# A two-layer decoder trunk on one core: q and k turned and split for two tiles of tokens at a time, transfers priced by two queues in the planner, pieces and instructions ordered anew

## The chip, the cores and the metric

The kernel runs on one core of one Trainium2 chip. The metric is the device time of one execution in microseconds; each figure for a kernel is the median of its runs. For the kernel before: 1321.85 us, median of 3 runs (1321.65 to 1322.69).

The core has five engines with a queue each, which run in order: TensorE (PE in the profile; its weight loads are PEld), VectorE (DVE), ScalarE (ACT), GpSimd (POOL) and SyncE (SP). TensorE writes PSUM; VectorE and ScalarE read it. Transfers (DMA) are issued here by SP and by POOL.

## What is computed

Two layers over 512 tokens of 1024 channels. Each layer normalises its input, projects it once to twelve parts, and runs two branches side by side:

```python
h = rmsnorm(x, norm_g)
proj = h @ w_in
aq, ak, av, az, bqk, bv, bi, bf, bo, bz, ga, gb = jnp.split(proj, idx, axis=-1)
# A: differential attention, 8 heads, two maps of 64 each, v of 128
q = rope(rmsnorm(two_map_heads(aq), q_norm_g), cos, sin)
k = rope(rmsnorm(two_map_heads(ak), k_norm_g), cos, sin)
oa = diff_attention(q, k, v, lam)            # softmax map 0 - lam * softmax map 1
oa = rmsnorm(oa, attn_norm_g) * (1.0 - lam_init)
ya = (oa * silu(az)) @ w_out_a
# B: mLSTM, 8 heads, q and k of 64 from a causal convolution of 4, v of 128
hb = mlstm_chunkwise(mq, mk, mv, i_pre, f_pre)
yb = (sigmoid(bo) * rmsnorm(hb, mlstm_norm_g) * silu(bz)) @ w_out_b
u = jax.nn.sigmoid(ga) * ya + jax.nn.sigmoid(gb) * yb
return x + u @ w_o
```

## The kernel before

**Products.** Every float32 product is made of three: each operand is split into a rounded high part and the rest (`split`, L522: ScalarE casts, VectorE subtracts), and `mm3` (L526) adds high x high, high x low and low x high in PSUM. Weights come from memory in pieces of 128 x 1024 floats (512 KB). A piece is loaded by SP into `wr`, cast by ScalarE to `wh`, and VectorE makes the rest `wl`. A piece whose name is in the list `dlo` goes another way (`dload`, L1743): POOL loads it into `dh`, ScalarE writes its negative to `dl`, and a second POOL transfer adds the piece onto `dl`. That takes two slots of the pool `qkp` (24 slots); where there is no room, the piece goes the first way. `dla` says how many pieces ahead it is issued.

**Pieces.** Names are those of the parts: qk0 to qk3 (q and k of two heads each, four pieces), av0 and av1, az, ga, bqk, bo, bz, woa, wob (eight each), the gates. bv, gb and wo are made by seven products instead of eight (P1 to P7): for these, combinations of weights are formed by accumulating transfers on POOL or on VectorE (`tdve`, L1736; a sum counts as VectorE's only if the products that it stands between come in a given order), and combinations of the tokens (`lhS`, `llS`) are formed once for bv, written to memory (`dS1h` and so on, L781) and reloaded for gb (L804).

**q and k.** Per pair of heads and tile of 128 tokens, `qk_done` (L1014) takes the sums of squares and rotates into a tile `rot`. At the second tile of a pair of tiles it computes the norms of both and calls `qk_back` and `qk_split` (L1077) for each of the two. `qk_split` queues a step `back`, `qkt` = 5 steps later, which turns the tile with four transposes into one PSUM bank (`qkt`) and takes it apart: `A.copy` of q's half into `qs`, the rest by VectorE, `A.copy` of k's half twice (`ks`), its rest into `kl`. All of these are 64 partitions x 256. `qkn` tells the attention heads how many tiles are there.

**Attention and mLSTM heads** are chains of steps (L1378) with start times (`a0`, `ap`, `m0`, `mp`) and offsets (`attn`, `ml`). A head's first step waits until the head before it has come to step `gateA` or `gateM`. `actp` names the query blocks whose scaling by the softmax sums is ScalarE's, the others are VectorE's. Per head the sum of squares of the output is a product with ones: for heads in `foldA` and `foldM` the two halves of partitions are added first and one product is made (`fold`, L1494), for others the high and low part take two (L1504). The mLSTM steps `decay` and `expm` broadcast rows of gate values from memory (`dd`, `em`).

**Order.** Nothing runs while the kernel is written down: a `Recorder` keeps every operation with its predecessors, and `schedule` (L298) plays them through with prices and picks, engine by engine, the startable operation with the smallest key: its nominal TensorE time, plus a `bias` by the name of its output, plus penalties (`group` for a change between small and large matmuls, `drain`, `late`). SP keeps the recorded order. `issue` (L467) then emits all in that order, which fixes every engine's queue; so every instruction bears L474 in the profile.

The price of a transfer, in nanoseconds, with one line for all queues (`rate`, L288, is in bytes per nanosecond: 360 from memory, 250 from the chip, 175 for rows, 150 accumulating):

```python
go = s + c if e == "POOL" else s
dma = max(dma, go) + size / self.rate(o)
end[i] = max(dma, go) + (5500.0 if e == "POOL" else 5000.0 if o["a"][1].tensor.name.startswith("rows") else 3000.0)
```

## Time and profile before

| | before |
|---|---|
| median of 3 runs | 1321.85 us |
| the profiled execution | 1324.05 us, span 1322.3 us |
| mean granted TensorE clock | 0.999 |
| busy: TensorE, VectorE, ScalarE, POOL | 1310.4, 1068.1, 959.0, 88.7 us |
| moved by DMA | 192.25 MB |

The span runs from the first to the last instruction. A matmul's end is modelled, so a busy TensorE can still be waiting for a short time. Views used below: the table of busy time, busy time in stretches of 33 us, groups of instructions of one operation and tile (count, busy time, mean time of one, idle time of the engine before them and what ended it), the chain of work that ended last (start, duration, what), the timeline, the waits, and the transfers with the median time from issue to landing.

### The profile page before, as it was taken

How to read it: one execution, taken by the hardware profiler on the slowest of the kernel's cores; microseconds unless marked ns; L12 is line 12 of the kernel's file. 1: busy time of each engine (PE TensorE's matmuls, PEld its weight loads, DVE VectorE, ACT ScalarE, POOL GpSimd, SP SyncE). 2: the span in 40 equal slices, each digit the busy share in tenths (PEclk: the TensorE clock that was granted, in tenths of full speed). 3: DMA queues.
4: the chain of work that ended last, by engine and by line, in shares of the span. 5: the costliest groups of instructions: out<-in, count | busy, mean ns of one | idle time of the engine just before them, and what ended most of it. 6: DMA issues, size and time to landing. Idle time of an engine off the chain costs nothing.

```text
span 1322.3 us, 18461 instructions
## 1 busy us (share of the span) xinstructions
PE 1310.4 (99%) x6436; PEld 1096.2 (83%) x6436; DVE 1068.1 (81%) x1890; ACT 959.0 (73%) x1940; POOL 88.7 (7%) x112
## 2 busy tenths in 40 slices
PE   9999999999999999999999999999999999999998
PEld 7888888888888788998888888888888887889886
DVE  7898878797668879967888988788965888797686
ACT  5888789896457768863668887888944677697643
POOL 1000000000010100010100100000001101101100
PEclk9999999999999999999999999999999999999999
DMA  5222232226676557776844222321367655588755
GB/s 189 73 80 83 93 100 74 83 65 175 210 207 167 158 139 185 229 212 146 290 136 123 62 81 82 94 88 58 103 172 253 182 154 143 127 204 275 192 139 191
DMA packets 63373, 192.25 MB, mean 145 GB/s; under 512 B 7440, under 2 KB 14224, under 8 KB 63280
## 3 DMA queue, kind: packets, MB, share of 16 engines
q1 hardware_dynamic: 51184, 147.02, 34.6%
q0 software_dynamic: 12096, 44.05, 15.7%
q8 instruction: 51, 0.84, 0.2%
q14 instruction: 42, 0.34, 0.1%
HBM read 178.39 MB, written 12.65 MB: 144 GB/s over the span
## 4 chain that ended last, share of the span: by engine, by line
PE 89%; DMA 4%; ACT 3%; DVE 2%; issue 1%; SPq 0%; DVEq 0%; ACTq 0%
PE qk L474 13%; PE av L474 9%; PE az L474 7%; PE ga L474 7%; PE woa L474 7%; PE bqk L474 7%; PE wob L474 7%; PE wo_P L474 6%; PE bz L474 5%; PE bv_P L474 5%; PE bo L474 5%; PE gb_P L474 3%; PE sc L474 3%; DMA wr<-in_wp_dram 2%; DMA llS_gb<-dS3l 1%; PE ut L474 1%
## 5 line engine op out<-in xcount | busy, mean ns | idle before, releaser
L474 DVE TENSOR_TENSOR wl<-wr,wh 128x1024 fp32r<-128x1024 f32 (+1 forms) x176 | 209.8, 1196 | 46.4 <-ACT wh L474 41.8
L474 ACT CAST wh<-wr 128x1024 fp32r<-128x1024 f32 (+1 forms) x174 | 181.2, 1043 | 71.9 <-DMA wr<-in_wp_dram 25.6
L474 ACT ACTIVATE p<-sc,mx,rq 128x128 f32<-128x128 f32 (+3 forms) x128 | 78.5, 617 | 11.8 <-DVE mx L474 8.5
L474 PE MATMUL qk<-wl,hh 128*128 128x512 f32 x240 | 85.4, 398 | 0.5 <-DVE wl L474 0.5
L474 PE MATMUL qk<-wh,hl 128*128 128x512 f32 x240 | 84.9, 397 | 0.1
L474 PE MATMUL qk<-wh,hh 128*128 128x512 f32 x240 | 84.2, 397 | 0.8 <-ACT hh L474 0.8
L473 ACT ACT_TABLE_LOAD x61 | 78.3, 1283 | 1.1
L474 PE MATMUL woa<-oa,wh 128*128 128x512 f32 x224 | 72.4, 392 | 0.0
L474 PE MATMUL wob<-ob,wh 128*128 128x512 f32 x192 | 59.5, 390 | 0.0
L474 ACT CAST ks<-qkt 64x256 fp32r<-64x256 f32 x128 | 47.1, 368 | 10.9 <-DVE qs L474 8.7
L474 POOL DMA_DIRECT2D dl<-in_wp_dram x24 | 20.9, 872 | 495.4 <-ACT dl L474 466.5
L474 PEld LDWEIGHTS qk<-wh,hh 128*128 128x128 f32 x240 | 45.4, 189 | 9.7 <-ACT hh L474 1.0
L474 PEld LDWEIGHTS qk<-wl,hh 128*128 128x128 f32 x240 | 45.0, 189 | 9.8 <-DVE wl L474 0.9
L474 PEld LDWEIGHTS qk<-wh,hl 128*128 128x128 f32 x240 | 45.2, 189 | 9.4 <-DVE hl L474 0.4
L474 DVE TENSOR_REDUCE mx<-sc 128x2 f32<-128x256 f32 (+1 forms) x64 | 52.3, 817 | 0.7
L474 PEld LDWEIGHTS woa<-oa,wh 128*128 128x128 f32 x224 | 41.7, 188 | 8.4
L474 DVE SCALAR_TENSOR_TENSOR cv<-bqk,par,cv 128x509 f32<-128x509 f32 (+2 forms) x48 | 35.8, 746 | 13.2 <-ACT cv L474 12.3
L474 PE MATMUL az<-hh,wh 128*128 128x512 f32 x112 | 44.7, 399 | 0.0
L474 ACT ACTIVATE sq<-qk 128x64 f32<-128x64 f32 (+1 forms) x144 | 36.5, 266 | 11.0 <-PE qk L474 10.3
L474 PE MATMUL az<-hh,wl 128*128 128x512 f32 x112 | 44.5, 397 | 0.0
L474 PE MATMUL ga<-hh,wh 128*128 128x512 f32 x112 | 44.4, 396 | 0.0
L474 PE MATMUL az<-hl,wh 128*128 128x512 f32 x112 | 44.4, 396 | 0.0
(400 smaller groups left out, 4147.8 us busy)
## 6 DMA issues: line engine op xcount, KB each, us to landing
wr<-in_wp_dram SPq DMA_DIRECT2D x172, 512.0 KB, 3.6
dh<-in_wp_dram POOLq DMA_DIRECT2D x24, 512.0 KB, 6.4
dl<-in_wp_dram POOLq DMA_DIRECT2D x24, 512.0 KB, 6.7
wws_wo<-in_wp_dram POOLq DMA_DIRECT2D x12, 512.0 KB, 7.4
dd<-rows SPq DMA_DIRECT2D x16, 256.0 KB, 4.1
wws_bv<-in_wp_dram POOLq DMA_DIRECT2D x8, 512.0 KB, 6.8
em<-rows SPq DMA_DIRECT2D x16, 256.0 KB, 7.2
wws_gb<-in_wp_dram POOLq DMA_DIRECT2D x8, 512.0 KB, 10.2
```

Source lines behind the costliest of these rows:

```text
L473: self.tc.keep_in_program_order(self.nc.scalar.preload_act_table_set(self.SET_NAME[o["load"]]))
L474: self.tc.keep_in_program_order(getattr(o["e"], o["fn"])(*o["a"], **o["k"]))
```

## The change

`qk_split` stores a tile and returns; at the second of two it queues two steps, one for q (side 0) and one for k (side 1, one step later). Each turns its half of both tiles by four transposes into one PSUM bank, and each cast or subtraction then covers 64 partitions x 512. `qk_done` and `qk_load` are adapted (`qk_load` isn't used, since `qspill` is empty):

```diff
         def qk_split(c, tt, rq):
+            st[("rot", c, tt % 2)] = rq
+            if tt % 2 == 0:
+                return
+            rqs = [st[("rot", c, t)] for t in range(2)]
+            def back(side):
+                def f():
+                    if side and ("qkq", c, tt) not in st:
+                        return False
+                    pst = ps_tr.tile([P, 2, 2, P], F32, tag="tr", name=f"qkt{side}{l}_{c}_{tt}")
+                    for t in range(2):
+                        for g in range(2):
+                            T.transpose(pst[:, g, t, :], rqs[t][:, (2 * side + g) * P : (2 * side + g + 1) * P], ident)
+                    ts = slice((tt - 1) * P, (tt + 1) * P)
+                    L, H = slice(0, 64), slice(64, 128)
+                    src = pst.rearrange("p g t k -> p g (t k)")
+                    for r, (a, b) in enumerate(((L, H), (H, L))):
+                        t = st[("qs", c)][2 * side + r][:, :, ts]
+                        A.copy(t[a], src[a])
+                        if side:
+                            A.copy(t[b], src[a])
+                            t2_, o = st[("kl", c)][r][:, :, ts], a
+                        else:
+                            t2_, o = t, b
+                        V.tensor_tensor(t2_[o], src[a], t[a].bitcast(F32), ALU.subtract)
...
+            for side in range(2):
+                defer(TUNE["qkt"] + side, back(side))
```

The price of a transfer becomes that of two queues (SP and POOL) that share while both have work:

```diff
         if o["k"].get("accum_op") is not None:
+            return 190.0
+        if o["eng"] == "POOL":
+            return 480.0
+        if src.space == DRAM and src.tensor.name.startswith("rows"):
             return 150.0
-        return 175.0 if src.tensor.name.startswith("rows") else 250.0 if src.space != DRAM else 360.0
+        return 380.0 if src.space == DRAM and math.prod(list(o["a"][0].shape)) >= 131072 else 310.0
+    def land(self, o, go, queue):
...
+        w = size / self.rate(o)
+        own = 0.55 if z else 0.45
+        t = max(go + (100.0 if z else 350.0), queue[z])
+        r = queue[1 - z] - t
+        if r <= 0:
+            fin = t + w
+        elif w / own <= r / (1.0 - own):
+            d = w / own
+            fin = t + d
+            queue[1 - z] = fin + (r - d * (1.0 - own))
+        else:
+            d = r / (1.0 - own)
+            queue[1 - z] = t + d
+            fin = t + d + (w - d * own)
+        queue[z] = fin
+        return fin + (2300.0 if z else 1850.0)
```

The table `TUNE` gets new values: the order of pieces, offsets and penalties, and a new `bias` for nearly every name. Those that change which instructions run, or when heads may start:

```diff
-        "qk0 av0 gate az0 qk1 az1 az2 av1 qk2 az5 ga4 qk3 az3 az4 ga3 az7 ga7 ga6 bqk4 ga2 bqk5 az6 ga1 ga0 woa7 woa3 "
+        "qk0 av0 gate az0 qk1 av1 az1 az2 qk2 az5 ga6 qk3 az3 az4 ga3 az7 ga2 ga0 bqk4 ga5 bqk5 az6 ga7 ga4 woa7 woa3 "
...
-    "attn": (0, 4, 5, 10, 13, 15, 15, 16, 20, 26),
+    "attn": (0, 3, 7, 10, 14, 14, 15, 16, 20, 28),
-    "foldM": (0, 1, 2, 3, 4, 5),
+    "foldM": (1, 3, 4, 5),
-    "gateA": 1,
-    "gateM": 4,
-    "actp": (0, 1, 2, 3),
+    "gateA": 6,
+    "gateM": 1,
+    "actp": (1, 2, 3),
-    "dlo": ('az0', 'az2', 'az6', 'bo1', 'bo4', 'bo6', 'bo7', 'bqk3', 'bz3', 'ga3', 'gb1', 'gb4', 'qk0.3', 'qk1.2', 'woa4', 'wob1', 'wob5'),
-    "dla": 5,
+    "dlo": ('az0', 'az2', 'az3', 'az6', 'bo1', 'bo4', 'bo6', 'bo7', 'bqk3', 'bz3', 'ga3', 'gb1', 'gb4', 'qk0.3', 'qk1.2', 'qk2.0', 'woa0', 'woa4', 'woa6', 'wob1', 'wob5'),
+    "dla": 6,
-    "tdve": {'bv': ('T2', 'T4'), 'wo': ('T1', 'T3'), 'gb': ('T2', 'T4')},
+    "tdve": {'bv': ('T2', 'T4'), 'wo': ('T2', 'T3'), 'gb': ('T2', 'T4')},
-    "group": 2214.6,
+    "group": 524.6,
-    "risk": 182.7,
-    "late": 33.8,
+    "risk": 11511209765781.4,
+    "late": 196689.9,
```

With the new `risk` the penalty `late` falls on every operation alike.

More of the change, by code (lines that the diff above doesn't have):

```diff
@@ L38 @@
     "order": (
[4 rows of a table removed]
[4 rows of a table added]
     ),
     "qkt": 5,
-    "gct": 13,
-    "gls": 2,
-    "glf": 7,
-    "attn": (0, 4, 5, 10, 13, 15, 15, 16, 20, 26),
+    "gct": 11,
+    "gls": 3,
+    "glf": 4,
+    "attn": (0, 3, 7, 10, 14, 14, 15, 16, 20, 28),
     "a0": 24,
@@ L51 @@
     "a4": 20,
-    "ml": (0, 6, 12, 14, 25, 38),
+    "ml": (0, 5, 12, 12, 25, 37),
     "ahead": 3,
-    "lc": 5,
-    "slack": 38.3,
+    "lc": 6,
+    "slack": 175.0,
     "margin": 0.0,
-    "pemargin": 123.8,
-    "wait": 278.0,
+    "pemargin": 140.8,
+    "wait": 208.2,
     "swpen": 141896579.9,
-    "smargin": 466.2,
+    "smargin": 634.6,
     "pwait": 0.0,
-    "wdiff": 6830.8,
+    "wdiff": 6373.2,
     "wsp": 4,
@@ L72 @@
     "acl": 7,
-    "gateA": 1,
-    "gateM": 4,
-    "actp": (0, 1, 2, 3),
+    "gateA": 6,
+    "gateM": 1,
+    "actp": (1, 2, 3),
     "m0": 228,
     "mp": 14,
-    "m4": 6,
+    "m4": 5,
     "slots": 24,
-    "hfd": 20,
+    "hfd": 22,
     "tset": (0, 18),
@@ L88 @@
     "qspill": {},
[3 rows of a table removed]
-    "drain": 62.6,
-    "group": 2214.6,
[3 rows of a table added]
+    "drain": 58.1,
+    "group": 524.6,
     "lates": ('bv', 'gb'),
-    "risk": 182.7,
-    "late": 33.8,
+    "risk": 11511209765781.4,
+    "late": 196689.9,
 }
@@ L291, in rate @@
         if o["k"].get("accum_op") is not None:
+            return 190.0
+        if o["eng"] == "POOL":
+            return 480.0
+        if src.space == DRAM and src.tensor.name.startswith("rows"):
             return 150.0
-        return 175.0 if src.tensor.name.startswith("rows") else 250.0 if src.space != DRAM else 360.0
+        return 380.0 if src.space == DRAM and math.prod(list(o["a"][0].shape)) >= 131072 else 310.0
+    def land(self, o, go, queue):
+        z = int(o["eng"] == "POOL")
+        size = 4.0
+        for x in list(o["a"][0].shape):
+            size *= x
+        w = size / self.rate(o)
[14 more added lines that the diff above has]
+        return fin + (2300.0 if z else 1850.0)
     LAT = {("ACT", "DVE"): 131, ("ACT", "PE"): 262, ("ACT", "ACT"): 153, ("DVE", "ACT"): 130, ("DVE", "PE"): 240, ("DVE", "DVE"): 127,
@@ L343, in schedule @@
         end = [0.0] * n
-        dma = 0.0
+        queue = [0.0, 0.0]
         table = 6
@@ L426, in schedule @@
             if o["fn"] == "dma_start":
-                size = 4.0
-                for x in list(o["a"][0].shape):
-                    size *= x
-                go = s + c if e == "POOL" else s
-                dma = max(dma, go) + size / self.rate(o)
-                end[i] = max(dma, go) + (5500.0 if e == "POOL" else 5000.0 if o["a"][1].tensor.name.startswith("rows") else 3000.0)
+                end[i] = self.land(o, s + c if e == "POOL" else s, queue)
             for t in o["tiles"]:
@@ L1003, in f @@
             def f():
-                if ("qd", c, tt) not in st or tt and st.get(("qkn", c), 0) < tt or not tt and not room(6):
+                if tt % 2 == 0:
+                    return
+                if ("qd", c, tt) not in st or tt > 1 and st.get(("qkn", c), 0) < tt - 1 or tt == 1 and not room(6):
                     return False
-                if not tt:
+                if tt == 1:
                     qk_take(c)
-                rq = t2(f"rl{l}_{c}_{tt}")
-                SY.dma_start(rq, st["qd", c, tt])
-                qk_split(c, tt, rq)
+                for t in (tt - 1, tt):
+                    rq = t2(f"rl{l}_{c}_{t}")
+                    SY.dma_start(rq, st["qd", c, t])
+                    qk_split(c, t, rq)
             return f
@@ L1058, in qk_done @@
             V.tensor_tensor(rqv, y, t, ALU.mult)
+            back = [st[("rot", c, t % 2)] for t in (tt - 1, tt)]
             for t in (tt - 1, tt):
-                qk_back(c, t, st[("rot", c, t % 2)])
+                qk_back(c, t, back[t % 2])
         def qk_back(c, tt, rq):
@@ L1077, in qk_split @@
         def qk_split(c, tt, rq):
-            def back():
-                pst = ps_tr.tile([P, 4, P], F32, tag="tr", name=f"qkt{l}_{c}_{tt}")
-                for g in range(4):
-                    T.transpose(pst[:, g, :], rq[:, g * P : (g + 1) * P], ident)
-                ts = slice(tt * P, (tt + 1) * P)
-                q0, q1, k0, k1 = (t[:, :, ts] for t in st[("qs", c)])
-                kl0, kl1 = (t[:, :, ts] for t in st[("kl", c)])
-                L, H = slice(0, 64), slice(64, 128)
-                for q, k, kl, a, b in ((q0, k0, kl0, L, H), (q1, k1, kl1, H, L)):
-                    A.copy(q[a], pst[a, 0:2, :])
-                    V.tensor_tensor(q[b], pst[a, 0:2, :], q[a].bitcast(F32), ALU.subtract)
-                    A.copy(k[a], pst[a, 2:4, :])
-                    A.copy(k[b], pst[a, 2:4, :])
-                    V.tensor_tensor(kl[a], pst[a, 2:4, :], k[a].bitcast(F32), ALU.subtract)
-                st[("qkn", c)] = tt + 1
@@ L1095, in qk_split @@
-            defer(TUNE["qkt"], back)
+            st[("rot", c, tt % 2)] = rq
+            if tt % 2 == 0:
+                return
+            rqs = [st[("rot", c, t)] for t in range(2)]
[19 more added lines that the diff above has]
+                        V.tensor_tensor(t2_[o], src[a], t[a].bitcast(F32), ALU.subtract)
+                    if side:
+                        st[("qkn", c)] = tt + 1
+                    else:
+                        st["qkq", c, tt] = 1
+                return f
```

10 rows, old and new, of the table TUNE are left out of this document.

## The prediction

> **What bounds the kernel now.** I read the page's table of busy time first, then busy time by stretches of 33 us, then the chain that ended last inside the stretches where TensorE pauses.
>
> ```profile
> span 1322.3 us, 18461 instructions
> PE 1310.4 (99%) x6436; PEld 1096.2 (83%) x6436; DVE 1068.1 (81%) x1890; ACT 959.0 (73%) x1940; POOL 88.7 (7%) x112
> 0.00:33.00 33.00, 29.83 (x125) 23.23 (x126) 24.16 (x67) 19.58 (x47) 4.95 (x9) 0.95 0.56 190
> 33.00:66.00 33.00, 33.00 (x159) 27.37 (x159) 28.22 (x73) 27.78 (x81) 0.00 (x0) 1.00 0.23 73
> 66.00:99.00 33.00, 33.00 (x167) 27.10 (x166) 32.05 (x80) 28.05 (x75) 0.95 (x1) 1.00 0.24 81
> ...
> 363.00:396.00 33.00, 32.66 (x144) 26.42 (x143) 22.52 (x27) 18.45 (x25) 6.18 (x8) 1.00 0.75 205
> 429.00:462.00 33.00, 32.19 (x151) 25.92 (x150) 28.23 (x41) 24.55 (x38) 3.34 (x4) 1.00 0.57 156
> 528.00:561.00 33.00, 32.83 (x235) 30.54 (x234) 30.46 (x43) 30.16 (x42) 1.72 (x2) 1.00 0.75 229
> 561.00:594.00 33.00, 32.67 (x222) 30.30 (x222) 22.57 (x27) 21.97 (x28) 6.36 (x8) 1.00 0.75 216
> ...
> 1023.00:1056.00 33.00, 32.66 (x146) 26.59 (x145) 26.69 (x34) 20.03 (x26) 4.80 (x7) 1.00 0.66 189
> 1089.00:1122.00 33.00, 32.00 (x148) 25.67 (x147) 28.36 (x42) 25.04 (x38) 3.35 (x4) 1.00 0.52 142
> 1188.00:1221.00 33.00, 32.13 (x251) 30.88 (x251) 26.34 (x34) 23.85 (x33) 3.49 (x4) 1.00 0.80 264
> 1221.00:1254.00 33.00, 32.55 (x195) 28.97 (x194) 21.10 (x27) 21.95 (x30) 4.64 (x6) 1.00 0.71 190
> 1287.00:1322.30 35.30, 30.86 (x135) 24.89 (x133) 23.76 (x28) 11.75 (x13) 1.73 (x2) 1.00 0.61 196
> ```
>
> In a stretch's row the first pair after the stretch is TensorE's busy time, the fourth VectorE's (DVE), the fifth ScalarE's (ACT); the last three columns are granted clock, DMA share and GB/s. TensorE bounds: it is idle for 1322.3 - 1310.4 = 11.9 us in all. The rows say where. The first 33 us lose 3.17. The last 35.3 lose 4.44. The eight rows between lose 0.34 + 0.81 + 0.17 + 0.33 + 0.34 + 1.00 + 0.87 + 0.45 = 4.31. All other stretches read 33.00 of 33.00, also 66:99, where VectorE works 32.05 of 33 us: there VectorE is nearly full, and still nothing of it reaches TensorE.
>
> A busy time can hide part of a wait, so the spacing of matmuls matters:
>
> ```profile
> 1294.54 0.50 PE L474 MATMUL wo_P<-wh,uhB 128*128 128x512 f32 x1 [0.78 <-DVE xr L474]
> ...
> 1295.33 0.40 PE L474 MATMUL wo_P<-wh,uhZ 128*128 128x512 f32 x1
> 1295.34 0.19 PEld L474 LDWEIGHTS wo_P<-wl,uhZ 128*128 128x128 f32 x1
> ...
> 1295.57 0.39 PE L474 MATMUL wo_P<-wl,uhZ 128*128 128x512 f32 x1
> ```
>
> A matmul is shown for 0.39 us, but the next starts 0.23 us after it. A wait shows as idle only beyond 0.16 us. The Trainium skill ("Perfetto Trace Analysis", Identifying the Most-Contended Engine) warns that matmul busy share is no measure of headroom, and that the share of weight loads is; by it the 83% would leave 17%, some 220 us. The trace disagrees: a load of 0.19 in a spacing of 0.23 is 0.83 by itself, and in 66:99, with no wait, loads take 27.10 of 33, or 0.82. So 83% is this program's full rate; I give a gain beyond the waits 2 in 100.
>
> What ended the largest of the waits:
>
> ```profile
> 442.33 8.09 DMA wr<-in_wp_dram
> ...
> 451.46 1.53 ACT dd L474 x3
> ...
> 453.01 1.24 DVE dd L474
> ...
> 454.38 0.48 PE ms L474 x2
> 560.90 8.85 DMA llS_gb<-dS3l
> 1184.11 11.07 DMA llS_gb<-dS1l
> 1213.78 9.19 DMA llS_gb<-dS3l
> L474 PE MATMUL gb_P<-llS_gb,wh 128*128 128x256 f32 x128 | 33.4, 287 | 1.4 <-DMA llS_gb<-dS3l 0.8 <-DMA llS_gb<-dS1l 0.6
> 376.77 1.14 DVE llS_bv L474
> ```
>
> A late weight load (wr) held ScalarE's cast; the decay exponentials of an mLSTM head (dd) stood behind that cast, and TensorE waited for them. The same place in layer 1 gives the 1.00 of 1089:1122. The reloaded token combinations llS_gb cost 1.4 us by their own row: 0.33 in 561:594 and 0.45 in 1221:1254 on dS3l, 0.64 of the 0.87 in 1188:1221 on dS1l. So transfers make 0.81 + 1.00 + 0.33 + 0.64 + 0.45 = 3.23 us in five waits; with the hidden 0.16 of each, **4.0 us**. The rest, 0.34 twice at llS_bv, 0.78 at xr and some 0.4 elsewhere, is VectorE's or ScalarE's: 1.9 us, with six hidden parts 2.9.
>
> **The change part by part.** *Turning q and k.*
>
> ```profile
> L474 ACT CAST ks<-qkt 64x256 fp32r<-64x256 f32 x128 | 47.1, 368 | 10.9 <-DVE qs L474 8.7
> L474 ACT CAST qs<-qkt 64x256 fp32r<-64x256 f32 x64 | 23.5, 367 | 11.4 <-PE qkt L474 5.6 <-DVE kl L474 4.5
> L474 DVE TENSOR_TENSOR qs<-qkt,qs 64x256 fp32r<-64x256 f32 x64 | 27.0, 422 | 11.7 <-ACT qs L474 10.3
> L474 DVE TENSOR_TENSOR kl<-qkt,ks 64x256 fp32r<-64x256 f32 x64 | 26.9, 421 | 10.5 <-ACT ks L474 8.9
> L474 ACT ACTIVATE ms_b<-num 64x512 f32<-64x512 f32 x12 | 7.0, 581 | 0.0
> L474 DVE TENSOR_TENSOR mql<-cv,mq 64x512 fp32r<-64x512 f32 x16 | 11.0, 685 | 1.8 <-ACT mq L474 1.3
> ```
>
> The 192 casts and 128 subtractions become 96 and 64 of twice the width. At 0.58 and 0.69 us (the two 64x512 rows) ScalarE goes from 70.6 to 55.7 us and VectorE from 53.9 to 44.2: 15 and 10 us less. The 128 transposes on TensorE stay 128, still four to a PSUM tile. Both engines' savings fall in stretches that read 33.00 of 33.00, so they are worth **0**; the cover is TensorE's own queue. The added wait is small: both tiles of a pair were already queued together, and the k side now stands one step behind the q side. Behind it on TensorE stand the scores of the next head, which the rows show never waited for.
>
> *Smaller edits.* Heads 0 and 2 of the mLSTM are no longer folded before their sum of squares: one matmul more per head and layer, four of 0.23 = **+0.9 us** straight on TensorE, the one certain cost. (It spares VectorE and ScalarE an instruction of 0.58 to 0.69 us in each.) The first scaling of an attention block (0.40 us each, below) goes from ScalarE to VectorE, sixteen times; at most 0.4 x 16 = 6.5 us on VectorE, less than the 10 it is spared: 0, or the whole 6.5 if that were all exposed, which I exclude by 66:99. T1 for T2 in the list for wo does nothing: both need an order of products that wo's sequence doesn't have. Moving av1 right behind qk1 puts two pieces of four accumulators side by side, as qk0 and av0 stand now; 33:66 holds that pair and shows no idle: 0.
>
> *More weights through POOL.* Four more names (az3, qk2.0, woa0, woa6) take the path of two POOL transfers instead of one SP load, a cast and a subtraction: up to 8 pieces in two layers.
>
> ```profile
> L474 ACT ACTIVATE p<-p,sums 128x128 f32<-128x128 f32 x16 | 6.5, 404 | 0.2
> L474 DVE TENSOR_TENSOR wl<-wr,wh 128x1024 fp32r<-128x1024 f32 (+1 forms) x176 | 209.8, 1196 | 46.4 <-ACT wh L474 41.8
> POOL dl L474 <- ACT dl L474: 466.5, 23, 44.2
> wr<-in_wp_dram SPq DMA_DIRECT2D x172, 512.0 KB, 3.6
> dl<-in_wp_dram POOLq DMA_DIRECT2D x24, 512.0 KB, 6.7
> ```
>
> VectorE is spared 8 x 1.2 = 9.6 us, 0 on the path. SP loses 8 loads, POOL gets 16 issues. POOL runs in order, and each accumulation waits there for ScalarE's negated copy, up to 44.2 us; behind it stand the zero fills of kl and mql and the sums for bv, gb and wo. Cost: 0 while those are as early as now; at worst one wait like the largest idle above, 1.0 us, per layer. I take 0, nearest to the 33.00 of the attention stretches. The bytes grow by 8 x 0.5 = 4 MB of 192. The Trainium skill ("DMA: Bandwidth & Descriptors", Issuing engines are not separate DMA queues) says that transfers of all issuers share the same 16 engines, so a second queue brings no rate; that the one row above is nearly twice the other agrees. By this rule the sum would only gain those bytes, spread over both layers.
>
> *The price of transfers in the plan, and the new order.* This alone can touch the 4.0 us. The planner sets every engine's order from prices. The old price runs all transfers in one line and adds 3.0 us (SP) or 5.5 (POOL); the new one has two lines that share, and adds 0.35 + 1.85 (SP) or 0.1 + 2.3 (POOL). For a lone 512 KB load that is 524288/360 = 1.46 + 3.0 = 4.5 us before and 1.38 + 2.2 = 3.6 after; the median row says 3.6. So the new price is nearer on the whole, and has no margin. At the wait of 454 us it doesn't help:
>
> ```profile
> 440.47 1.75 SPq L474 DMA_DIRECT2D dd<-rows  x4
> 442.33 0.36 SPq L474 DMA_DIRECT2D wr<-in_wp_dram  x1
> ```
>
> Four broadcasts of 640 KB, then the load. Old: 440.47 + 3.74 + 1.46 + 3.0 = 448.7; new: 440.47 + 0.35 + 4.37 + 1.38 + 1.85 = 448.4; landed: 442.33 + 8.09 = 450.4. Both are 2 us early. What speaks for a gain all the same is that the order around each of these places is drawn anew, with biases for dd, wl and the bv and gb pieces changed, and that a wait needs a coincidence: five of over 200 transfers (172 loads of wr and 24 of dl in the rows above alone) are seen on TensorE. The bounds for this part: all seen waits go, 4.0 + 2.9 = -6.9; or new ones come, +3.5 (below). I take -4.0, the transfers' share; the other 2.9 is VectorE's and ScalarE's order, whose prices don't change.
>
> **Sum**, against the profiled execution's 1324.05 us (span 1322.3 and 1.75 around it): -4.0 + 0.9 = -3.1, so 1320.95. The median of the runs, 1321.85, lies 2.2 below that execution, so I expect **1318.7** in such runs. About 0.2% (2.6 us) is what a measurement of this kernel can tell from no change; the forecast is at -0.24%.
>
> **Rivals.** (1) *Waits are swapped.* The five waits go and five like them come elsewhere: +0.9 alone, 1322.8. For it: the price is as early as before at 454 us. Against: fewer instructions on both engines. (2) *Reloads arrive after the plan*, the case of the other side. The place is the gb stage, four reloaded combinations in each layer. The plan now expects a lone reload 0.9 us sooner (4.5 against 3.6), while the three rows above show 8.9 to 11.1. TensorE is in order, so if it is let up to the planned landing, each reload costs the difference: 8 x 0.9 = 7.2 at most; half of them, +3.5, with +0.9 and all old waits left: 1326.3. It decides once a reload lands over 0.16 us behind TensorE's turn. For it: both old prices were short there already. Against: ordering by readiness puts other work in front. (3) *All waits between start and end go*, helped by engines that have 25 us less to do: -6.9 + 0.9, 1315.9. Against: start and end waits have other causes. (4) *The relief is not there*: 64x512 instructions cost twice the 64x256 ones. VectorE then keeps 10 us more in full stretches; TensorE, never waiting there, shows nothing, and the time is that of the forecast or of (1).
>
> **How the numbers follow.** Forecast 0.40, swapped waits 0.30, late reloads 0.20, all waits gone 0.10; (4) lies within the first two. The forecast's own range, 1317.0 to 1320.5, crosses the border at 1319.2, so a quarter of it counts as no change, against some of (1) that ends beyond it: faster 0.44, same 0.34, slower 0.22. For 8 in 10 the range takes in case (3) with 1 us for the start, and (2): 1314.8 to 1326.5. Faster and slower cases together hold 0.66, hence the forecast's own range beside it.
>
> **What would show it.** Right: 96 casts and 64 subtractions at 0.58 and 0.69; four more msp_b matmuls; no idle before ms at 454 and 1106 us; TensorE's busy time within 1 us of 1311. Wrong: idle before gb_P released by llS_gb that exceeds today's 1.4 us (case 2), idle in the attention stretches (then POOL's queue or the q and k relief matters), or a change in the first 33 us, which I hold fixed.

## The result and the profile after

The changed kernel takes **1330.5 us** (median of six runs, 1328.4 to 1335.3) where the kernel before took 1322.1 beside it (1321.7 to 1322.8): a ratio of 1.0069, 95% interval 1.0049 to 1.0089. It is slower by 8.4 us; 1318.7 was forecast, and the range ended at 1326.5. The execution in its profile took 1328.72 us, with a span of 1327.0. Of all runs behind the figures below one, the slowest of seven of the kernel called e5, took 4642.36 us where the other six took 1318.3 to 1320.4; the ratios leave it out.

First the page's head, busy times and chain of the changed kernel:

```profile
span 1327.0 us, 18355 instructions
...
PE 1310.5 (99%) x6440; PEld 1095.3 (83%) x6440; DVE 1051.6 (79%) x1831; ACT 950.6 (72%) x1836; POOL 98.0 (7%) x126
...
PE 88%; DMA 7%; DVE 2%; ACT 1%; SPq 1%; issue 0%; DVEq 0%; ACTq 0%
```

TensorE's busy time reads as it was (1310.4 before). VectorE and ScalarE have less to do, as the change means them to: 16.5 and 8.4 us. So the growth of the span, 4.7 us, is all but 0.1 us TensorE's idle time: 16.5 us where it was 11.9.

The two profiles hold only part of the 8.4 us. TensorE's clock is one reason. In the execution of the kernel before it ran at half clock from 12.7 to 16.1 us, which added some 1.6 us to its busy time; that is the 0.95 in the first row of the prediction, where the row below has 1.00. One of these microseconds, of the kernel before (the third column from the end is the granted clock):

```profile
14.00:15.00 1.00, 1.00 (x5) 0.82 (x5) 0.97 (x4) 0.94 (x4) 0.00 (x0) 0.50 0.87 356
```

At one clock the spans would differ by some 6.3 us, and TensorE's busy time by some 1.7 (an estimate: 4.7 and 0.1, each with the 1.6). The other 2 us of the 8.4 are in no profile here.

Where the idle time lies is read from the stretches of 33 us (the columns are those of the prediction):

```profile
0.00:33.00 33.00, 30.05 (x131) 23.57 (x132) 25.21 (x74) 20.25 (x45) 4.63 (x9) 1.00 0.58 205
...
297.00:330.00 33.00, 31.44 (x145) 25.63 (x144) 23.73 (x32) 18.21 (x29) 1.71 (x2) 1.00 0.55 134
...
429.00:462.00 33.00, 32.90 (x157) 27.30 (x156) 27.80 (x41) 28.43 (x42) 3.49 (x5) 1.00 0.42 120
...
660.00:693.00 33.00, 30.92 (x151) 25.60 (x150) 25.50 (x50) 18.94 (x50) 2.30 (x3) 1.00 0.55 158
957.00:990.00 33.00, 32.01 (x147) 26.35 (x146) 24.35 (x29) 17.91 (x24) 2.57 (x3) 1.00 0.46 129
...
1056.00:1089.00 33.00, 31.54 (x147) 26.11 (x146) 25.14 (x37) 22.27 (x31) 2.29 (x3) 1.00 0.93 195
1089.00:1122.00 33.00, 33.00 (x156) 27.36 (x155) 28.94 (x42) 28.50 (x42) 3.34 (x4) 1.00 0.50 138
...
1221.00:1254.00 33.00, 31.66 (x209) 28.89 (x208) 18.89 (x24) 20.25 (x27) 5.58 (x8) 1.00 0.86 231
```

The two waits before ms at 454 and 1106 us are gone, as forecast: 429:462 lost 0.81 and now loses 0.10, 1089:1122 lost 1.00 and now nothing. In their place stretches that read 33.00 of 33.00 have lost 1.56, 2.08, 0.99 and 1.46 us, the last again before an ms, at 1074 us. The chain inside the largest:

```profile
666.12 9.18 DMA wr<-in_wp_dram
675.29 0.02 issue
675.32 1.05 ACT wh L496
...
676.42 0.50 PE qk L496
```

The chain inside the first, and the transfers that end two more:

```profile
299.25 7.56 DMA dd<-rows
...
306.91 0.42 DVE dd L496
307.33 0.21 DVE ul L496
...
307.59 0.72 PE av L496 x3
1060.83 10.69 DMA dd<-rows
1218.90 10.04 DMA llS_gb<-dS3l
```

Each of these waits goes back to a transfer. At 674 us a weight load lands 9.18 us after its issue and ScalarE's cast waits for it. At 306 us VectorE stands before a mask sum dd whose broadcast has not landed; the subtraction ul behind it, which needs nothing of that broadcast, is what TensorE waits for. Waits that go back to transfers now make 1.56 + 0.99 + 1.46 (dd) + 0.53 + 2.08 (wr) + 1.34 (llS_gb) = 8.0 us of visible idle time, 3.2 before: the difference is the 4.7. Half of the 8.0 are broadcasts (dd). The table of waits says the same of the other engines, first after (engine and what it waited for: us in all, times, longest), then before:

```profile
ACT wh L496 <- DMA wr<-in_wp_dram: 43.2, 16, 8.6
...
DVE dd L496 <- DMA dd<-rows: 14.3, 13, 3.5
```

```profile
ACT wh L474 <- DMA wr<-in_wp_dram: 25.6, 12, 5.0
```

**Plan against trace.** The planner gives every transfer a landing time, and the trace has the real one. Set one beside the other, with TensorE's own lag behind the plan at that point taken off (it ends at 15.4 us before, 23.0 after), and count the transfers whose landing the trace shows by itself (all of POOL's, and half of SP's: 179 of 359 before, 176 of 352 after):

```
kernel   plan's end   transfers   behind the plan   by > 1 us   by > 2 us   median
before      1307.7         263                27           6           1   -1.86 us
after       1303.9         274               117          56          24   -0.17 us

transfers on SP without broadcasts    n   median   > 1 us behind   issue to landing, median / longest
before, POOL's queue empty           86    -1.19          2              3.56 / 10.50
before, POOL transfers in flight     60    -1.11          4              5.87 / 12.56
after,  POOL's queue empty           58    -0.20          2              3.54 /  9.48
after,  POOL transfers in flight     67    +0.78         28              6.82 / 12.17

broadcasts on SP, before             33    -2.59          0              5.61 /  8.97
broadcasts on SP, after              51    -0.10         12              6.43 /  9.42
POOL's own, before                   84    -4.92          0              7.04 / 14.08
POOL's own, after                    98    -0.43         14              7.02 / 14.31
```

The new price promised 3.8 us (the plan's end), and at its last matmul TensorE stood 7.6 us further behind the plan. The price is right for a load with POOL's queue empty. With POOL transfers in flight it is too early for 28 of 67. Broadcasts lost more: they landed 2.6 us ahead of the old plan in the median and land with the new one, 12 of 51 over 1 us behind it.

### The profile page after: what moved, and what is told of

Same layout as the page of the kernel before. It is cut to its first block, busy times and chain, and to the rows that moved or that the text cites. A ratio compares the mean times of both kernels' runs of the same rounds, so it can differ in the third digit from the quotient of the medians.

```text
span 1327.0 us, 18355 instructions
## 1 busy us (share of the span) xinstructions
PE 1310.5 (99%) x6440; PEld 1095.3 (83%) x6440; DVE 1051.6 (79%) x1831; ACT 950.6 (72%) x1836; POOL 98.0 (7%) x126
## 4 chain that ended last, share of the span: by engine, by line
PE 88%; DMA 7%; DVE 2%; ACT 1%; SPq 1%; issue 0%; DVEq 0%; ACTq 0%
PE qk L496 12%; PE av L496 8%; PE az L496 7%; PE ga L496 7%; PE wob L496 7%; PE bqk L496 7%; PE bz L496 6%; PE woa L496 6%; PE bv_P L496 5%; PE wo_P L496 5%; PE gb_P L496 5%; PE bo L496 5%; DMA dd<-rows 4%; PE sc L496 3%; PE num L496 2%; DMA wr<-in_wp_dram 2%
## 5 line engine op out<-in xcount | busy, mean ns | idle before, releaser
L496 ACT CAST wh<-wr 128x1024 fp32r<-128x1024 f32 x167 | 173.5, 1045 | 122.5 <-DMA wr<-in_wp_dram 43.2
L496 DVE TENSOR_TENSOR wl<-wr,wh 128x1024 fp32r<-128x1024 f32 (+1 forms) x169 | 200.9, 1195 | 63.3 <-ACT wh L496 58.7
L496 PE MATMUL woa<-oa,wh 128*128 128x512 f32 x192 | 63.6, 390 | 0.0
L496 PE MATMUL av<-wh,hh 128*128 128x512 f32 x128 | 50.4, 398 | 0.4 <-DVE sq L496 0.4
L496 PE MATMUL av<-wl,hh 128*128 128x512 f32 x128 | 50.6, 397 | 0.0
L496 PE MATMUL av<-wh,hl 128*128 128x512 f32 x128 | 50.5, 398 | 0.0
L496 ACT ACTIVATE sq<-qk 128x64 f32<-128x64 f32 (+1 forms) x144 | 36.3, 270 | 16.5 <-PE qk L496 16.0
L496 PE MATMUL ga<-hl,wh 128*128 128x512 f32 x112 | 44.3, 396 | 0.0
L496 PE MATMUL bqk<-hh,wh 128*128 128x512 f32 x112 | 44.0, 393 | 0.0
L496 PE MATMUL bqk<-hh,wl 128*128 128x512 f32 x112 | 44.0, 393 | 0.0
L496 PE MATMUL ga<-hh,wl 128*128 128x512 f32 x112 | 43.9, 395 | 0.0
## 6 DMA issues: line engine op xcount, KB each, us to landing
wws_gb<-in_wp_dram POOLq DMA_DIRECT2D x8, 512.0 KB, 10.9
```

Of the source, the lines that this page charges most:

```text
L496: self.tc.keep_in_program_order(getattr(o["e"], o["fn"])(*o["a"], **o["k"]))
```

## The experiments

**Theory A**: the price has no margin, so the plan puts a consumer where the transfer is due; half land later, and engines that work in order pass each wait on. **Rivals**: B, the turn for two tiles; C, any new order is worse; D, the further POOL pieces. An order follows from the price, so a price can't be exchanged under a fixed order: for e1, e2, e5 to e9, e11, e12 and e14 to e17 the biases and offsets in `TUNE`, the penalties and, within bounds, the order of the pieces were searched anew, judged by the plan's end, or, in e8, e12 and e17, by replays with late landings. Ratios are to the kernel before, run beside each.

```
run                             price   plan's end  >1 us behind  time     ratio (95% interval)
before                          old        1307.7      6/263     1322.1
after                           new        1303.9     56/274     1330.5   1.0069 (1.0049-1.0089)
e1  turn alone                  old        1305.9     13/263     1321.8   1.0001 (0.9991-1.0011)
e2  price alone                 new        1304.0     39/266     1336.0   1.0108 (1.0094-1.0122)
e3  after, dl short             new        1303.9     40/274     1324.8   1.0020 (1.0011-1.0029)
e4  after, dd behind ul         new        1303.9     53/274     1331.7   1.0078 (1.0063-1.0093)
e5  all but the price           old        1305.8     11/274     1319.4   0.9976 (0.9965-0.9987)
e6  margin 1 us                 new+1.0    1305.5     25/366     1325.7   1.0027 (1.0018-1.0036)
e7  margin 2 us                 new+2.0    1310.6     20/366     1332.9   1.0077 (1.0063-1.0091)
e8  turn alone, replays         old+0.07   1309.3     10/308     1320.7   0.9990 (0.9981-0.9999)
e9  all but the price, 2nd      old        1307.2      9/272     1326.5   1.0034 (1.0022-1.0046)
e10 e7, wws_gb short            new+2.0    1310.6     13/366     1322.0   1.0001 (0.9992-1.0010)
e11 margin 1 us, 2nd            new+1.0    1305.5     35/366     1328.6   1.0047 (1.0034-1.0060)
e12 all but the price, replays  old+0.08   1311.9     11/318     1323.5   1.0015 (1.0005-1.0025)
e13 e9, reload ahead            old        1307.2      7/272     1328.6   1.0038 (1.0024-1.0052)
e14 new price, 2nd search       new        1303.8     66/366     1347.9   1.0194 (1.0169-1.0220)
e15 new price, 3rd search       new        1305.6     39/321     1351.6   1.0222 (1.0208-1.0235)
e16 all but the price, 3rd      old        1307.5      9/276     1328.6   1.0053 (1.0041-1.0066)
e17 margin 2 us, replays        new+2.08   1311.9     21/366     1334.9   1.0101 (1.0084-1.0118)
e18 e17, reload ahead           new+2.08   1311.9     15/366     1324.0   1.0017 (1.0006-1.0028)
```

### One part alone: e1 and e2

In the diffs `...` stands for lines left out.

```diff
-            def back():
-                pst = ps_tr.tile([P, 4, P], F32, tag="tr", name=f"qkt{l}_{c}_{tt}")
...
+            def back(side):
...
+                    pst = ps_tr.tile([P, 2, 2, P], F32, tag="tr", name=f"qkt{side}{l}_{c}_{tt}")
...
```

> The kernel before with one part of the change alone: q and k turned and split for two tiles at a time. The price of transfers is the old one, the list of pieces through POOL is the old one; the biases and offsets are searched anew for this program under the old price (without that the same edit leaves a plan 5.6 us longer). The plan ends at 1305.9 us by its own account (before: 1307.7). Theory A (the new price has no margin, so the transfers land behind the plan): no harm here, 1318 to 1322, the runs within 1.5 us of each other as before's are, and few waits on transfers. Rival B (the turn for two tiles makes the harm, by the longer instructions or by k standing a step behind q): 1327 or more, with TensorE idle in the attention stretches. Rival C (any order fitted anew is worse than the old one on the chip): 1325 or more, with waits of all kinds.

```diff
-        return 175.0 if src.tensor.name.startswith("rows") else 250.0 if src.space != DRAM else 360.0
+        return 380.0 if src.space == DRAM and math.prod(list(o["a"][0].shape)) >= 131072 else 310.0
...
+    def land(self, o, go, queue):
...
```

> The kernel before with the other part alone: the new price of transfers, with the turn one tile at a time and the old list of pieces through POOL; biases and offsets searched anew under the new price. The plan ends at 1304.0 us (the changed kernel: 1303.9). Theory A: slower, 1327 to 1333, runs spread over 3 us or more, and transfers that land behind the plan: waits of ACT wh on DMA wr and of DVE dd on DMA rows grow from 25.6 and about 0 us to above 35 and 8. Rival B (turn): as before, 1319 to 1323, since no turn is changed. Rival D (the eight further pieces through POOL make the contention): as before too. Rival C: 1325 or more, but with waits of VectorE and ScalarE on each other rather than on transfers.

The turn alone changes nothing that can be measured: rival B falls. The price alone costs more than the whole change, 13.7 us, and more than the 1327 to 1333 expected: D falls as the sole cause, since e2 has the old list of pieces. Its waits on broadcasts came as expected, 11.8 us; those on wr grew less (29.9 us, above 35 expected):

```profile
ACT wh L491 <- DMA wr<-in_wp_dram: 29.9, 14, 5.0
DVE dd L491 <- DMA dd<-rows: 11.8, 11, 2.4
```

### The changed kernel's order, one thing taken away: e3 and e4

```diff
+            a = list(o["a"])
+            if o["k"].get("accum_op") is not None and o["kind"] in ('dl',):
+                a = [x[:, 0:64] for x in a]
...
```

> The changed kernel in its exact order; the 31 accumulating transfers of the low part of the weights (dl on POOL) move only the first 64 of 1024 columns, so the rest of the low part is left out and 15.2 MB less are moved. Rival D (POOL's pieces contend with SP's loads and make the harm): most of the 8.4 us goes, 1322 to 1324. Theory A: only the waits go that lie beside such a piece (the 2.1 us at 674 us in the changed kernel's profile, perhaps part of the 0.5 at 370): 1326 to 1329, while the waits of dd at 306, 962 and 1072 us and that of llS_gb at 1227 stay, 4 to 5 us together.

1324.8: more than half of the loss went, 5.7 us, between the two theories. By the profile the wait at 674 us fell from 2.08 to 0.77, that at 1072 from 1.46 to 0.58, and that at 1227 (1.34) went; those for broadcasts at 306 and 962 us stayed, 1.46 and 1.57. The wait at 674 us, in the changed kernel and then in e3:

```profile
676.42 0.50 PE L496 MATMUL qk<-wh,hh 128*128 128x512 f32 x1 [2.08 <-ACT wh L496]
```

```profile
675.54 0.50 PE L499 MATMUL qk<-wh,hh 128*128 128x512 f32 x1 [0.77 <-ACT wh L499]
```

So these 31 transfers on POOL make more than half of the loss. They don't make all of the lateness: 40 of 274 transfers still land over 1 us behind the plan (56 without the edit), and two waits for broadcasts stay.

```diff
+        for d, u in ((3050, 2521), (8141, 7612)):
+            order.remove(d)
+            order.insert(order.index(u) + 1, d)
```

> The changed kernel with two of VectorE's instructions moved: the mask sums dd that wait for the last piece of the broadcast rows, at 306 us and at 962 us, stand behind the subtraction ul that they held up, which the av matmuls need. Nothing else is changed. If TensorE's waits there (0.45 + 1.11 and 0.99 us) come from a waiting instruction that stands in front of a ready one on an in-order engine, as Theory A has it, they go and the time falls by 2 to 3 us, to 1327.5 to 1328.5. If the time there was lost because the scores themselves were late (the rows come too late whatever stands behind), the same wait shows at ms, the matmul behind dd, and the time stays at 1330.5.

A miss: 1331.7, nearer to the second outcome, though not by its reason. The profile tells why. The av matmuls no longer wait; the broadcast still lands 7.35 us after its issue, and the wait comes back a few instructions later:

```profile
299.50 7.35 DMA dd<-rows
...
306.94 0.44 DVE dd L499
...
310.05 0.63 ACT fo_a L499
...
311.53 0.47 PE msp_a L499
```

There TensorE waits 0.93 us where it waited 1.56, at 969 us 0.52 for 0.99: 1.1 us won of 2.55. And the wait at 674 us, which nothing in this edit touches, came out at 2.78 us, and with it something new. Stretches of 1 us; the third column from the end is the granted clock:

```profile
675.00:676.00 1.00, 0.00 (x0) 0.00 (x0) 0.00 (x0) 0.00 (x0) 0.00 (x0) 1.00 1.11 395
676.00:677.00 1.00, 0.00 (x0) 0.00 (x0) 0.00 (x0) 0.89 (x1) 0.00 (x0) 1.00 1.06 385
677.00:678.00 1.00, 0.79 (x6) 0.72 (x6) 0.81 (x1) 0.15 (x1) 0.00 (x0) 1.00 1.06 414
678.00:679.00 1.00, 1.00 (x8) 0.89 (x6) 0.82 (x3) 0.59 (x1) 0.00 (x0) 0.57 0.85 348
679.00:680.00 1.00, 1.00 (x5) 0.81 (x4) 0.52 (x2) 0.59 (x1) 0.00 (x0) 0.50 0.76 94
680.00:681.00 1.00, 1.00 (x4) 0.81 (x3) 1.00 (x4) 0.00 (x0) 0.00 (x0) 0.50 0.81 319
681.00:682.00 1.00, 1.00 (x5) 0.81 (x4) 0.47 (x3) 0.00 (x0) 0.00 (x0) 0.72 0.30 119
```

TensorE is shown fully busy, but at half clock: 0.43 + 0.50 + 0.50 + 0.28 = 1.7 us lost behind a wait of 2.8. This counts as busy time on the page; the last section comes back to it.

### The price taken back: e5, e8, e9, e12, e13, e16

```diff
-        return fin + (2300.0 if z else 1850.0)
...
-                end[i] = self.land(o, s + c if e == "POOL" else s, queue)
...
+                dma = max(dma, go) + size / self.rate(o)
+                end[i] = max(dma, go) + (5500.0 if e == "POOL" else 5000.0 if o["a"][1].tensor.name.startswith("rows") else 3000.0)
```

> The changed kernel with everything of the change but the price: the turn for two tiles, the longer list of pieces through POOL, the folds as changed; only the price of transfers is the old one again, with biases and offsets searched anew under it. The plan ends at 1305.8 us by its own account, 1.9 us later than the changed kernel's 1303.9. Theory A (the price): the harm is gone, 1317 to 1322, although the plan is longer; few transfers land behind it. Rival D (the further pieces through POOL make the contention, whatever the price): 1326 to 1331. Rival B (turn) is already refuted by the turn alone at 1321.75 and would need 1327 or more here.

> Again everything of the change but the price, from another search under the old price, with the products of bv in the same sequence as in the changed kernel (in the first such kernel product P7 stood behind P4, which changes what is computed in bv, not its amount). The plan ends at 1307.2 us, 3.3 us later than the changed kernel's. Theory A: 1318 to 1322, few transfers more than 1 us behind the plan. If the 1319.4 of the first was owed to that sequence: 1326 or more.

> The whole change but the price, a third search under the old price; its plan ends at 1307.5 us, later than both of the new price's. If the price sets the time: 1318 to 1325. If the search does: anything from 1319 to 1336.

Three searches gave 1319.4, 1326.5 and 1328.6: the first as expected, the others behind Theory A's range. The 1326.5 is the outcome that e9's expectation named for the case that e5 owes its time to its own sequence of bv's products; the three orders with the changed kernel's sequence (e9, e16, and e12 below) take 1323.5 to 1328.6, so that case is not excluded. All three are slower than the kernel before, by ratios of 1.0015 to 1.0053: under the old price the rest of the change is no gain in them, and how the 8.4 us divide between it and the price stays open. e2, which has the price alone, is free of this.

Nine to eleven of the counted transfers land more than 1 us behind the plan in each of e5, e9 and e16, so the count doesn't tell them apart. But it leaves out half of SP's transfers, and in e16's profile (1332.8) the two longest waits behind the start go back to such loads:

```profile
365.55 13.23 DMA wr<-in_wp_dram
...
643.06 14.32 DMA wr<-in_wp_dram
```

They landed 2.5 and 6.1 us behind the plan; TensorE waited 1.94 and 2.33 us, with half clock behind each. So single late loads make at least part of e16's time, under the old price too. In e9 one place in each layer stood out:

```profile
1186.82 10.34 DMA lhS_gb<-dS1h
```

TensorE waited 1.93 and 1.73 us for this reload, with half clock behind each. It stood behind four broadcasts on SP; e13 puts it ahead of them:

```diff
+        for d, u in ((4146, 4066), (9237, 9157)):
+            order.remove(d)
+            order.insert(order.index(u), d)
```

> The second kernel with everything of the change but the price, in its exact order; on SP's queue one reload in each layer, lhS_gb from dS1h, stands ahead of the four broadcasts of rows that it followed. Nothing else is changed. In that kernel TensorE waited 1.93 and 1.73 us for it, the reload landing 10.3 us after its issue, and the granted clock was 0.5 for 3.4 us behind each wait. If this one place makes the excess over the first such kernel: 1.93 + 1.73 + twice 1.7 = 7.1 us less, 1319 to 1321. If the excess is spread, or the broadcasts are then late in its place: 1324 or more.

The median is 1328.6, so the second outcome came: this one place does not make the excess. In the profiled execution (1323.1; e9's took 1329.1) TensorE's waits there fell to 0.64 and 0.86 us, now for the next reload, with no loss of clock, and behind the start there is no other wait above 0.8. Three of the nine runs, with a mean clock of 1.000, lie at 1323.1 to 1324.5; the other six, at 0.997 to 0.999, at 1327.5 to 1330.3. So some wait turns up in most runs that the profiled one doesn't show. Which one stays open, and so does the rest of what parts the searches under one price.

> A try for a version that beats both: the kernel before with the turn for two tiles, old price plus 0.07 us, and the order searched not for the shortest plan but for the shortest mean over replays of the plan in which landings are late by a random part (a mean of 0.56 us over all, 3 us and more for 4 in 100). The plan ends at 1309.3 us by its own account, later than all others. Theory A: 1315 to 1320, below the 1321.75 of the turn alone whose plan was 3.4 us shorter. A theory by which the plan's own length decides expects 1325.

> A closing version: the whole change but the price, old price plus 0.08 us, the order searched for the shortest mean over replays with landings late by a random part. The plan ends at 1311.9 us, 8.0 us later than the changed kernel's. Theory A: 1317 to 1321, faster than both kernels. A theory by which the plan's own length decides expects 1330 or more.

Both have later plans than e9 and e16 and are faster: the plan's length does not decide. e12 missed its range by 2.5 us, e8 by 0.7. e8 beats the kernel before with nothing changed in what is computed, by 1.3 us, at the edge of what can be told (0.1 to 2.5 by the interval); of e5 and e6 this can't be said, since the products of their bv stand in another sequence.

### A margin on the new price: e6, e11, e7, e10, e17, e18

```diff
-        return fin + (2300.0 if z else 1850.0)
+        return fin + (3300.0 if z else 2850.0)
```

> The changed kernel with its new price and 1.0 us added to every landing (1.85 to 2.85 us on SP, 2.3 to 3.3 on POOL), biases and offsets searched anew; the plan ends at 1305.5 us with the margin in it. In the changed kernel's profile 56 of 274 transfers land more than 1 us behind the plan; Theory A expects the waits of all but those to go: 1322 to 1326. If the missing margin is not the cause, the margin buys nothing: 1329 to 1333.

> The changed kernel with 1.0 us added to every landing, another search, with the products of bv in the changed kernel's sequence (in the first such kernel P7 stood ahead of P2 and P6). The plan ends at 1305.5 us as in the first. Theory A: 1323 to 1328, as the 1325.7 of the first. If the margin buys nothing: 1329 to 1333.

With 1 us of margin 1325.7 and 1328.6, both below the 1330.5 and the 1336.0 without; the second missed its range by 0.6 us, and its interval overlaps that of the changed kernel. With 2 us (4300 and 3850 in that line):

> As the last, with 2.0 us added to every landing; the plan ends at 1310.6 us, 6.7 us later than the changed kernel's by its own account. 24 of 274 transfers land more than 2 us behind the changed kernel's plan. Theory A: faster than the changed kernel all the same, 1319 to 1324. A theory by which the plan's own length decides expects 6 to 7 us more than the changed kernel, 1337.

A miss: 1332.9. One place in each layer holds it, the reload llS_gb<-dS3l. Its landing, and the issues around it:

```profile
563.21 11.40 DMA llS_gb<-dS3l
```

```profile
562.69 0.42 SPq L491 DMA_DIRECT2D wr<-in_wp_dram  x1
563.21 0.52 SPq L491 DMA_DIRECT2D llS_gb<-dS3l  x1
564.08 0.85 POOL L491 DMA_DIRECT2D wws_gb<-in_wp_dram  x1 [6.11 <-DVE wl L491]
565.22 0.86 POOL L491 DMA_DIRECT2D wws_gb<-in_wp_dram  x1 [0.29 <-DVE wl L491]
...
574.65 0.39 PE L491 MATMUL gb_P<-llS_gb,wh 128*128 128x256 f32 x1 [3.09 <-DMA llS_gb<-dS3l]
```

With TensorE's lag taken at the issue, the reload lands 3.6 us behind its planned time, margin included, and the two POOL accumulations issued behind it 1.0 and 1.4 us ahead of theirs. `land` cannot see this: it prices a transfer when it is placed, and the branch that lets two queues share moves the other queue's front, never a landing already given. Theory A' says so; e10 shortens those accumulations.

```diff
+            if o["k"].get("accum_op") is not None and o["kind"] in ("wws0_gb", "wws1_gb"):
+                a = [x[:, 0:64] for x in a]
...
```

> The kernel with 2.0 us added to every landing, in its exact order; the eight accumulations wws_gb on POOL move only the first 64 of 1024 columns (the rest of that weight combination is left out). In that kernel TensorE waited 3.09 and 3.21 us for the reload llS_gb<-dS3l, issued at 563.21 and landed 11.40 us later, 3.7 us behind its planned time with the margin, while two such accumulations were issued 0.9 and 2.0 us behind it; after both waits the granted clock was 0.5 for 3.4 us (1.7 us lost each time). Theory A', that the new model prices a landing when it is placed and never moves it for a transfer issued later on the other queue: both waits go, and the clock loss with them, 1332.9 - 6.3 - 3.4 = 1323, between 1322 and 1325, and the two reloads land 6 to 8 us after their issue. If SP's own queue makes the lateness: no change, 1331 or more.

1322.0, as A' has it. The landing is 8.2 us after the issue, and of TensorE's wait of 3.09 a wait of 0.21 before the weight load is left:

```profile
570.17 0.19 PEld L494 LDWEIGHTS gb_P<-llS_gb,wh 128*128 128x128 f32 x1 [0.21 <-DMA llS_gb<-dS3l]
```

> The whole change with the new price and 2.08 us added to every landing, the order searched for the shortest mean over replays with landings late by a random part; the plan ends at 1311.9 us, 8.0 us later than the changed kernel's. If the missing margin is the cause: 1319 to 1326, 5 to 11 us faster than the changed kernel. If the new price is worse in itself, with its two queues that share: 1328 or more.

Missed by the same place, further out: 1334.9, which is the outcome named for a price that is worse in itself. Waits of 3.73 and 5.47 us:

```profile
561.65 12.46 DMA llS_gb<-dS3l
...
1219.16 14.17 DMA llS_gb<-dS3l
```

Nothing else of note is left in that profile, and nothing has to be left out to test it:

```diff
+        for d, u in ((4589, 4418), (9680, 9509)):
+            order.remove(d)
+            order.insert(order.index(u) + 1, d)
```

> The order of e17 (new price and 2.08 us of margin), with one transfer moved on SP's queue in each layer: the weight load wr that stood ahead of the reload llS_gb from dS3l stands behind it. In e17 the reload landed 12.46 and 14.17 us after its issue, TensorE waited 3.73 and 5.47 us for it and the granted clock was 0.5 for 6.7 us behind each wait, 15.9 us in all; in the kernel before, with that sequence on SP and the same two accumulations on POOL behind it, the reloads of the gb stage landed 8.9 to 11.1 us after their issue. The consumer of the moved load stands 12 us behind that of the reload in the plan. If this one place holds the excess: waits of 0 to 1 us each and no clock loss, 1319 to 1322. If it is the price as such: 1330 or more.

One load moved in each layer took 10.9 us off, 1334.9 to 1324.0. It held 14.0 us, not the 15.9 of the expectation: half clock began 1.7 and 2.2 us before these waits ended, so that only 2.5 and 2.3 us of it fell on work. The first layer's wait is gone; in the second the reload still lands 11.19 us after its issue, and a wait of 2.31 with 1.7 us of clock remains, more than the 2 us by which the expectation was missed. POOL's accumulations are as they were, so what stands ahead on SP's own queue counts too.

```profile
1223.64 0.39 PE L494 MATMUL gb_P<-llS_gb,wh 128*128 128x256 f32 x1 [2.31 <-DMA llS_gb<-dS3l]
```

### The price or the luck of a search: e14 and e15

These change nothing in the changed kernel but what a search sets (biases, offsets, penalties and the order of pieces):

> The whole change, new price without margin, another search than the changed kernel's, begun from the order found with 1 us of margin; its plan ends at 1303.8 us (the changed kernel's: 1303.9). If the price sets the time: 1327 to 1336, like the two before. If it was the luck of the search: somewhere between 1319 and 1327, like the orders under the old price.

> As the last, from a search begun at an order of the old price; its plan ends at 1305.6 us. If the price sets the time: 1326 to 1335. If the search does: 1319 to 1327.

1347.9 and 1351.6, above even what Theory A expected. With no margin four orders give 1330.5, 1336.0, 1347.9 and 1351.6; under the old price seven (before, e1, e5, e8, e9, e12, e16) give 1319.4 to 1328.6. The groups don't overlap, which luck would do in 1 of 330 draws, if each order were a draw of its own (1 of 210 without e5). The price sets the group; within a group the search is worth up to 9 us under the old price and 21 under the new. Rival C holds in this smaller sense. The count of late transfers does not order the times within the new group either (56, 39, 66 and 39). In e15's profile the four longest waits behind the start, 3.31, 2.28, 2.27 and 1.81 us, all stand behind transfers: a load of wr, 10.17 us from issue to landing, and three broadcasts of 7.7 to 8.7.

## Why the prediction was wrong, step by step

*The bound and the turn: right.* TensorE's busy time came out at 1310.5 us, and the four matmuls of 0.9 us stand in the count (6440 for 6436). That it reads only 0.1 us more than before is luck: the execution before lost some 1.6 us to half clock. The turn's sizes came out to the digit:

```profile
L496 ACT CAST ks<-qkt 64x512 fp32r<-64x512 f32 x64 | 37.1, 579 | 6.6 <-PE qkt L496 3.0 <-DVE kl L496 2.8
...
L496 DVE TENSOR_TENSOR qs<-qkt,qs 64x512 fp32r<-64x512 f32 x32 | 22.0, 689 | 2.3 <-ACT qs L496 1.3
L496 DVE TENSOR_TENSOR kl<-qkt,ks 64x512 fp32r<-64x512 f32 x32 | 22.0, 687 | 16.0 <-ACT ks L496 15.6
L496 ACT CAST qs<-qkt 64x512 fp32r<-64x512 f32 x32 | 18.6, 581 | 9.4 <-PE qkt L496 4.7 <-DVE qs L496 4.4
```

55.7 us of casts and 44.0 of subtractions, 55.7 and 44.2 forecast; and they are worth 0, as e1 shows. Rival (4) is refuted by the same rows. That av1 behind qk1 costs 0 was off by 0.36 us, a wait at 110 us.

*More weights through POOL, taken at 0: the question was put too narrowly, and the size is open.* The bound asked whether POOL's own queue would be late. But POOL's transfers delay SP's: 5.7 us went when e3 shortened 31 of them. What the eight further pieces cost by themselves was not tried.

*The price and the new order, taken at -4.0: the step that failed.* The transfers' share of the waits did not go, it rose by 4.7 us, and the price alone cost 13.7 (e2). "The new price is nearer on the whole, and has no margin" is what the trace shows (a median of -0.20 us for loads with POOL's queue empty). The error is the conclusion: that lateness needs a coincidence, since five of over 200 transfers had been seen on TensorE. That count was taken under a price whose median load landed 1.2 us ahead of the plan, a broadcast 2.6 and a transfer of POOL's 4.9; this was the protection, and the change spends it. The two big waits it counted on did go; the transfers' share more than doubled, elsewhere. Whether the old price protects by what it adds or by having one line for both queues was not tried apart: with 2 us added to the new one (e7) still 20 of 366 transfers land over 1 us behind the plan, 6 of 263 before.

*The rival that was nearly right.* (2) had the mechanism, at 0.20, and was confined to the gb stage, with 0.9 us per reload, the difference of two lone loads. The waits came at wr and at broadcasts too, and beside POOL's transfers a landing is up to 7.0 us behind the plan, not 0.9. The sign named for it, more than 1.4 us of idle time at llS_gb, did not show (1.34); idle time in the attention stretches did, at 306 and 962 us, behind broadcasts. The rows of 8.9 to 11.1 us were in the prediction; they should have sized it. So should the upper end: the whole order is drawn anew, and its luck alone is worth several us.

## What to carry to other kernels

A cost model inside a static planner is not better for being closer to the median: where engines work in order, a landing that is planned too late costs a little everywhere, one too early stops an engine and what stands behind it. Before believing a shorter plan, set planned landings against those of a trace, apart for transfers alone and beside another queue; a margin is worth keeping where the second group is late. And when a long wait remains, look for the one transfer on its queue that could stand behind: a single swap was worth 10.9 us here.

## What the hardware showed that was not expected

*Half clock behind a wait.* The granted clock fell to 0.5 for about 3.4 us behind single TensorE waits, among them 1.93 and 1.73 us (e9), 2.18 and 2.47 (e2), 2.78 (e4), 2.31 (e18) and 3.09 and 3.21 (e7), and for 6.8 us at 3.73 and 5.47 (e17), there from 1.7 and 2.2 us before the wait's end; not behind 2.40 (e14), 2.08 (the changed kernel), 2.02 (e5) or 1.72 (e2). So in these runs a wait of 1.7 us or more could cost its length and 1.7 us more. Runs of one kernel differ in their clock: of the changed kernel's the slowest, 1335.3, has a mean of 0.996, the fastest 1.000. That such waits make the difference would fit, but only one run of each has a profile. The Trainium skill ("TensorE: Matmul & The Clock Gate", Why this matters for your kernels) warns of idle gaps above some 3 us; the two states, 1.0 and 0.5, agree with its account, but here much shorter gaps were enough.

*Two queues do not share evenly.* A load on SP with POOL's queue empty takes 3.5 us from issue to landing in the median, with POOL transfers in flight 6 to 7 and up to 14.7 (e16). At 1218 us of the changed kernel three loads on SP land 2.2, 4.6 and 7.0 us behind a plan that gives SP 45 parts in 100 and POOL 55, the two accumulations that POOL issued among them 0.3 and 0.6. The Trainium skill ("DMA: Bandwidth & Descriptors", Issuing engines are not separate DMA queues) says that all issuers end on the same engines; the trace agrees, and adds that a queue started later can overtake.
